# Two 128x128 by 256-column products that nobody reads, added to each of the 72 groups of a recurrence kernel

## The chip, the cores and the metric

The kernel runs on one core of one Trainium2 chip. The metric is device time in microseconds (us) of one execution; the time before is the median of 3 runs, 4142.04 us (4137.38 to 4148.01). Engines are named as the profile names them: PE is the matrix engine, PEld its weight loads, DVE, ACT and POOL the vector, scalar and general engines, SP the one that issues DMAs.

## The reference, cut to what matters

One layer of a trunk over 256 context and 2048 latent tokens of width 1024. A modulated norm and one input projection feed four mixers (mLSTM, RWKV-7, GLA, Gated DeltaNet) of 4 heads each. Every mixer scans the tokens forward and backward in chunks of 64; from chunk to chunk it carries a small state. For the DeltaNet heads, for example:

```python
def step(s, xs):
    u_c, w_c, k_c, ge = xs
    v_new = u_c - jnp.einsum('bhck,bhkv->bhcv', w_c, s)
    return jnp.exp(ge)[..., None, None] * s + jnp.einsum('bhck,bhcv->bhkv', k_c, v_new), s
```

The RWKV-7 step is of the same kind, with a triangular solve ahead of it. Then follow the output projection, a gated residual, a norm, a squared-ReLU MLP of width 4096, a second gated residual and a final norm:

```python
x = x + gate1_x * (mixed[:, n_ctx:] @ w_out[layer])
x = x + gate2_x * _mlp(_rms(x, norm2_w[layer]) * (1 + scale2_x) + shift2_x, mlp_w1[layer], mlp_w2[layer])
return _rms(x, final_norm_w)
```

## The kernel before, in words

**Dense work.** Every large product is split into a high and a low part in fp32r and made of three products of 128x128 weights by 512 (or 256) columns: `ps_z` is the input projection, `ps_o` the output projection, `ps_f` and `ps_a` the two halves of the MLP. `load_w` fetches a weight tile `w_f` by DMA, ACT makes `w_hi` of it and DVE or POOL `w_lo`.

**Rounds.** The tokens come in six rounds of chunks (`CHUNKS`). A round projects its tokens, prepares gates, decays and keys and writes them to DRAM; `solve` makes the triangular inverses of a chunk pair (`ps_n`, `ps_s`).

**Groups.** `group(d, c0)` makes one chunk of 64 tokens in one direction d for all four mixers: 36 chunks by 2 directions are 72 groups. Its products are in plain f32, 64x64 by 64 columns, of which two run on different halves of the array; each stands in the trace as two records. The chain from state to state is: products into `ps_R` from the old state `St`; then ACT copies columns 0 to 127 of it into `rR` and DVE makes `gR` of columns 128 to 255; products of both with the chunk's inverses (`X64`) into `ps_U`; ACT copies columns 0 to 255 into `U`; products into `ps_S`; POOL and DVE make the new `St`. `ps_R`, `ps_U` and `ps_S` are tiles of one pool tag, "ch", with one buffer of 128x512 f32, which is one PSUM bank: each of the three is opened when the readers of the one before are done. Columns 256 to 511 of `ps_R` and `ps_U` are not used. Beside the chain a group makes `ps_att` and `ps_ml` ahead of it, and the outputs `ps_ym` and `ps_ylgr` and, at its second direction, the norms and `ps_yT` behind it.

**What sets the order.** `interleave` in `body` writes the groups between the steps of the dense work: 48 of them during rounds 1 to 5, 24 during the first 35% of `tails`, the stage of output projection and MLP. What is written is then ordered by the tile framework: a planner plays the program through with its own costs (`schedule_with_timeline_sim=True`) and fixes, engine by engine, the order in which instructions stand; on the chip every engine runs its list in that order. `add_manual_dep(..., ORDER)` tells the planner that one instruction stands behind another on the same engine, without a wait. `self.ident` is a 128x128 identity, part of the constants' tile `pack`.

Of the kernel before, what the change touches and what calls it, by code (L numbers as in the profile page):

```python
# [166 lines left out]
ORDER = mybir.DependencyInfo(mybir.DependencyClass.NoSync, mybir.DependencyReason.DATA)  # L167
# [9 lines left out]
class Kern:  # L177
# [31 lines left out]
    def grp(self, t, par, mms):  # L209
# [6 lines left out]
                    self.tc.add_manual_dep(i.ins, p, ORDER, reason="one sum at a time in a bank")  # L216
        t.last[par] = i.ins.name

    def weave(self, t, mms):


        qs = [range(m[0].start // 32, m[0].stop // 32) for m in mms]
        left = collections.Counter(q for r in qs for q in r)
        for (rows, cols, l, r), quarters in zip(mms, qs):
            for q in quarters:
                left[q] -= 1
            prev = {t.last[q] for q in quarters if q in t.last}
            assert not prev or all(q in t.last for q in quarters)
            i = self.T.matmul(t.t[rows, cols], l, r, start=not prev, stop=not any(left[q] for q in quarters), skip_group_check=True)  # L229
            for p in prev:  # L230
                self.tc.add_manual_dep(i.ins, p, ORDER, reason="the first product of the bank's rows first")
            t.last.update({q: i.ins.name for q in quarters})
# [39 lines left out]
    def consts(self):  # L272
        A, c = self.A, self.ctx.enter_context(self.tc.tile_pool(name="const", bufs=1))
        self.cp = c
        pk = c.tile([128, sum(math.prod(x) for _, x in PACK)], F32, name="pack")
        self.dma(pk, A["pack"])
        v, o = {}, 0
        for k, x in PACK:
            w = math.prod(x)
            v[k] = pk[:, o:o + w]  # L280
            if len(x) == 2:
                v[k] = v[k].rearrange("p (a b) -> p a b", a=x[0])
            o += w
        self.vec = v
        self.ident, self.headsel, self.pairsel, rm = (v["k_" + k] for k in ("ident", "headsel", "pairsel", "rm"))
        self.rm64, self.rm16, self.rm4 = rm[:, 0:256], rm[:, 256:320], rm[:, 320:324]
        self.first = v["k_first"]
        for k in ("rw0", "ra0", "gconv", "nw"):
            self.ts(self.vec[k], self.vec[k], 0.5, ALU.mult)

        self.kah = c.tile([128, 2], F32, name="kah")
        self.ts(self.kah, self.vec["rka"], 0.5, ALU.mult)
        self.kac = c.tile([128, 2], F32, name="kac")
        self.ts(self.kac, self.kah, -1.0, ALU.mult, 1.0, ALU.add)

        self.rgn = c.tile([128, 2, 2, 128], F32, name="rgn")
        self.dma(self.rgn.rearrange("p x f d -> p (x f d)"), A["rgn"].to_broadcast([128, 512]))
        self.rc0 = c.tile([128, 8], F32, name="rc0")
        self.ts(self.rc0, self.vec["mup"], -1.0, ALU.mult, 1.0, ALU.add)
        self.tt(self.rc0, self.rc0, self.vec["mun"], ALU.subtract)  # L300
        self.mhalf = c.tile([128, 8], F32, name="mhalf")
        self.G.memset(self.mhalf, -0.5)
        self.ones = c.tile([128, 2], F32, name="ones")
        self.G.memset(self.ones, 1.0)
        self.pairq = c.tile([128, 2], F32, name="pairq")
        self.ts(self.pairq, self.pairsel, 32 ** -0.5, ALU.mult)
        self.reg = c.tile([128, 2, 2, NCH], F32, name="reg")
        self.leg = c.tile([128, 2, NCH], F32, name="leg")
        self.fs = [c.tile([128, NCH], F32, name=f"fs{d}") for d in range(2)]
# [1147 lines left out]
    def group(self, d, c0):  # L1457
# [9 lines left out]
        if hasq:  # L1467
            o, i = (13, 27) if d else (6, 0)
# [6 lines left out]
        r, i = self.part(c0)  # L1475
        i = X[f"rows{r}"][d, i].rearrange("h f k t -> h (f k t)")
        for h, p in enumerate(sl):
            self.dma(rw[p].rearrange("p f k t -> p (f k t)"), i[h:h + 1].to_broadcast([64, 640]))
        X64 = self.lt("t64", [2, 2, 64])
        i = X["t64"][d, c0 // 2].rearrange("p (m c w) -> p m c w", m=2, c=2)  # L1480
        self.dma(X64.rearrange("p m f t -> p m (f t)"), i[:, :, c0 % 2])
        tm = self.lt("tm", [1038])
        o = 332 if d else 0
# [7 lines left out]
        f2, g2 = sl, [slice(128, 192), slice(192, 256)]  # L1491
# [12 lines left out]
        b = self.bank(self.qa, "att", "ps_att", 1).t  # L1504
        rk = b[:, 0:256].rearrange("p (a t) -> p a t", t=64)
        ra, pk = (b[:, x:x + 128].rearrange("p (f t) -> p f t", f=2) for x in (256, 384))
# [37 lines left out]
        if hasq:  # L1544
# [4 lines left out]
            b = self.bank(self.qa, "att", "ps_ml", 1).t  # L1549
# [21 lines left out]
        def chb(nm):  # L1571
            return self.bank(self.qa, "ch", nm, 1)
        b = chb("ps_R")
# [2 lines left out]
        self.weave(b, [(p, f2[ft], Lt[p, 1 + ft], vr(ft)[p]) for ft, p in fp]  # L1576
                   + [(p, f2[ft], ff[p, 1 + ft], st[p, cr(ft)]) for ft, p in fp]
                   + [(p, g2[ft], kw[p, ft], st[p, f2[ft]]) for ft, p in fp])
        rR, gR = self.wt("rR", [128]), self.wt("gR", [128])
        self.act(rR, b.t[:, 0:128], AF.Copy)  # L1580
        self.tt(gR, vb, b.t[:, 128:256], ALU.add)
        b = chb("ps_U")
        for m, o, r in ((0, f2, rR), (1, g2, gR)):
            for ft, p in fp:
                self.mm(b.t[p, o[ft]], X64[p, m, ft], r[p, f2[ft]])

        U = self.wt("U", [256])
        self.act(U, b.t[:, 0:256], AF.Copy)
# [1 line left out]
        b = chb("ps_S")  # L1590
# [33 lines left out]
        for ms in ("m", "lgr"):  # L1624
            b = self.bank(self.qa, "yy", "ps_y" + ms, 1)
            first, then, last = [], [], []
            for mi, mm in enumerate(ms):
                w = 65 if mm == "m" else 64
                for ft, p in fp:
                    y = slice(128 * mi + w * ft, 128 * mi + w * ft + w)  # L1630
                    f, c, t, v = {"m": (Lq[:, 2 + ft], cm(ft), Lt[:, 6 + ft], vm(ft)), "l": (ff[:, 4 + ft], cl(ft), lS[:, ft], vl(ft)),
                                  "g": (Lq[:, ft], f2[ft], Lt[:, 4 + ft], U[:, g2[ft]]),
                                  "r": (ff[:, 3 * ft], cr(ft), Lt[:, 3 * ft], vr(ft))}[mm]
# [24 lines left out]
        else:  # L1658
            self.finish(yall, gat)
            b = self.psum("ps_yT", "yt" if "yt" in self.pb else "pp")  # L1660
# [271 lines left out]
```

## Time and profile before

| | |
|---|---|
| median of 3 runs | 4142.04 us |
| the profiled execution's own time | 4137.76 us |
| its span in the profile | 4136.0 us |
| PE busy | 3453.5 us (83%) |
| DVE, POOL, ACT busy | 2411.0, 1445.8, 1399.0 us |
| mean granted PE clock | 0.882 of full |

The span is the time between the first and the last recorded instruction; 1.8 us lie around it. "Busy" is the time in which an engine has an instruction under way, and PE's clock is told as the share of full speed that was granted. A pause of an engine is shown in brackets with what ended it.

### The profile page before, as it was taken

What the parts mean: (1) busy time and instruction counts of PE and PEld (TensorE: products, weight loads), DVE (VectorE), ACT (ScalarE), POOL (GpSimd) and SP (SyncE); (2) the same over time, 40 slices, a digit from 0 to 9 for tenths busy, and PEclk for the clock granted to TensorE, in tenths of its full rate; (3) what the DMA queues carried; (4) which work ended last, traced back from release to release, by engine and by line L of the source; (5) the groups of instructions that cost most, each with busy time, mean ns of one, the idle gap of its engine ahead of it and who ended that gap; (6) DMA issues with size and microseconds to landing.
All of it is one profiled execution on the core that took longest, in us unless ns stands there. A gap on an engine that the chain in (4) does not pass through costs nothing. (4 is left out here: it accounts for less than half of the span.)

```text
span 4136.0 us, 75041 instructions
## 1 busy us (share of the span) xinstructions
PE 3453.5 (83%) x29082; PEld 2794.0 (68%) x29082; DVE 2411.0 (58%) x5259; ACT 1399.0 (34%) x2544; POOL 1445.8 (35%) x1682
## 2 busy tenths in 40 slices
PE   6465878687777866568796999999999999999998
PEld 5344556566566755557685777777778778877886
DVE  6673875775587677536865645667653354335433
ACT  3334333443433433423332322233322332233222
POOL 3221735554345162502242423334422232223222
PEclk9667977877887886768898999999999999999999
DMA  5469577666776865757776544455622323232322
GB/s 203 112 182 146 107 157 182 162 133 157 146 158 138 196 140 144 171 142 196 195 215 183 160 123 143 139 153 150 196 91 97 114 94 124 97 107 92 104 97 86
DMA packets 609653, 592.68 MB, mean 143 GB/s; under 512 B 285664, under 2 KB 486448, under 8 KB 609296
## 3 DMA queue, kind: packets, MB, share of 16 engines
q1 hardware_dynamic: 609296, 587.87, 54.4%
q8 instruction: 230, 3.77, 0.4%
q14 instruction: 127, 1.04, 0.1%
HBM read 463.78 MB, written 123.92 MB: 142 GB/s over the span
## 5 line engine op out<-in xcount | busy, mean ns | idle before, releaser
L185 POOL TENSOR_TENSOR w_lo<-w_f,w_hi 128x1024 fp32r<-128x1024 f32 x213 | 511.6, 2402 | 1172.4 <-ACT w_hi L198 1086.2
L198 ACT ACTIVATE w_hi<-w_f 128x1024 fp32r<-128x1024 f32 (+1 forms) x427 | 448.0, 1051 | 956.8 <-PE ps_a L240 412.9
L185 DVE TENSOR_TENSOR w_lo<-w_f,w_hi 128x1024 fp32r<-128x1024 f32 (+1 forms) x214 | 269.8, 1261 | 248.4 <-ACT w_hi L198 245.8
L240 PE MATMUL ps_f<-h2h,w_hi 128*128 128x512 f32 x1024 | 404.5, 396 | 6.3 <-ACT w_hi L198 4.3
L240 PE MATMUL ps_a<-al,w_hi 128*128 128x512 f32 x1024 | 405.4, 396 | 0.0
L240 PE MATMUL ps_a<-ah,w_hi 128*128 128x512 f32 x1024 | 405.2, 401 | 0.0
L240 PE MATMUL ps_f<-h2h,w_lo 128*128 128x512 f32 x1024 | 404.8, 396 | 0.0
L240 PE MATMUL ps_a<-ah,w_lo 128*128 128x512 f32 x1024 | 402.6, 397 | 0.0
L240 PE MATMUL ps_f<-h2l,w_hi 128*128 128x512 f32 x1024 | 399.1, 394 | 3.5 <-DVE h2l L193 3.4
L240 PE MATMUL ps_z<-hh,w_hi 128*128 128x512 f32 (+3 forms) x760 | 306.2, 404 | 68.4 <-ACT hh L198 40.9
L193 DVE SCALAR_TENSOR_TENSOR x1T<-ps_a,modv,x1T 128x512 f32<-128x512 f32 x256 | 187.8, 748 | 279.9 <-PE ps_a L240 279.5
L240 PE MATMUL ps_z<-hh,w_lo 128*128 128x512 f32 (+3 forms) x760 | 301.1, 398 | 25.2 <-DVE w_lo L185 19.7
L240 PE MATMUL ps_z<-hl,w_hi 128*128 128x512 f32 (+2 forms) x760 | 294.8, 396 | 0.4 <-DVE hl L185 0.4
L240 PEld LDWEIGHTS ps_z<-hh,w_hi 128*128 128x128 f32 (+1 forms) x760 | 157.7, 208 | 110.2 <-ACT hh L198 46.1
L240 PEld LDWEIGHTS ps_f<-h2h,w_hi 128*128 128x128 f32 x1024 | 194.1, 190 | 51.4 <-ACT w_hi L198 6.9
L212 PE MATMUL ps_z<-w_hi,hh 128*128 128x256 f32 x672 | 206.3, 309 | 25.9 <-ACT w_hi L198 11.4
L240 PEld LDWEIGHTS ps_a<-ah,w_hi 128*128 128x128 f32 x1024 | 192.2, 188 | 50.0 <-DVE x1T L193 5.9
L240 PEld LDWEIGHTS ps_f<-h2l,w_hi 128*128 128x128 f32 x1024 | 193.8, 189 | 45.7 <-DVE h2l L193 4.7
L240 PEld LDWEIGHTS ps_a<-ah,w_lo 128*128 128x128 f32 x1024 | 192.5, 188 | 45.7 <-issue 0.5
L240 PEld LDWEIGHTS ps_f<-h2h,w_lo 128*128 128x128 f32 x1024 | 194.4, 190 | 41.4 <-DVE w_lo L185 0.5
L240 PEld LDWEIGHTS ps_a<-al,w_hi 128*128 128x128 f32 x1024 | 192.7, 188 | 43.8
L212 PE MATMUL ps_z<-w_lo,hh 128*128 128x256 f32 x672 | 203.3, 304 | 4.4 <-POOL w_lo L185 4.1
(430 smaller groups left out, 7835.1 us busy)
## 6 DMA issues: line engine op xcount, KB each, us to landing
w_f<-w SPq DMA_DIRECT2D x256, 512.0 KB
w_f<-wg SPq DMA_DIRECT2D x90, 512.0 KB
tm<-x_tm SPq DMA_DIRECT2D x144, 259.5 KB
kc<-x_fm SPq DMA_DIRECT2D x64, 448.0 KB
adaw<-ada SPq DMA_DIRECT2D x48, 512.0 KB
rw<-x_rows SPq DMA_DIRECT2D x144, 160.0 KB
w_f<-wp SPq DMA_DIRECT2D x44, 512.0 KB
w_f<-wout SPq DMA_DIRECT2D x32, 512.0 KB
```

The costliest lines, as they stand in the source:

```text
L185: return (e or self.V).tensor_tensor(out=o, in0=a, in1=b, op=op)
L193: return self.V.scalar_tensor_tensor(o, a, s, b, op0, op1)
L198: return self.S.activation(o, a, f, bias=bias, scale=scale)
L212: i = self.T.matmul(o, l, r, start=k == 0, stop=k == len(mms) - 1)
L240: return self.T.matmul(o, l, r, start=start, stop=stop)
```

## The change

A method `warm` is added. It makes one f32 product of the identity (128x128) with the first 256 columns of `pack`, into columns 256 to 511 of a bank that is just in use; no instruction reads them. A group calls it twice: behind the last product into `ps_R`, with all products into `ps_U` ordered behind it, and behind the last product into `ps_U`. What the kernel computes stays as it was.

```diff
+    def warm(self, t, after):
+
+        i = self.T.matmul(t.t[:, 256:512], self.ident, self.pack[:, 0:256], start=True, stop=True)
+        for p in after:
+            self.tc.add_manual_dep(i.ins, p, ORDER, reason="in the pause after")
+        return i.ins.name
...
+        self.pack = pk
...
         self.weave(b, [(p, f2[ft], Lt[p, 1 + ft], vr(ft)[p]) for ft, p in fp]
                    + [(p, f2[ft], ff[p, 1 + ft], st[p, cr(ft)]) for ft, p in fp]
                    + [(p, g2[ft], kw[p, ft], st[p, f2[ft]]) for ft, p in fp])
+        warm = self.warm(b, b.last.values())
         rR, gR = self.wt("rR", [128]), self.wt("gR", [128])
         self.act(rR, b.t[:, 0:128], AF.Copy)
         self.tt(gR, vb, b.t[:, 128:256], ALU.add)
         b = chb("ps_U")
         for m, o, r in ((0, f2, rR), (1, g2, gR)):
             for ft, p in fp:
-                self.mm(b.t[p, o[ft]], X64[p, m, ft], r[p, f2[ft]])
+                i = self.mm(b.t[p, o[ft]], X64[p, m, ft], r[p, f2[ft]])
+                self.tc.add_manual_dep(i.ins, warm, ORDER, reason="in the pause before")
+                b.last[ft, p.start, m] = i.ins.name
+        warm = self.warm(b, b.last.values())
```

The planner orders the whole program anew, so rows move on all engines, on SP too, by a few places each; no tile, pool or DMA is added or taken away. The first place is PE's list in one of the last groups before `tails`. Before:

```order
L229 MATMUL ps_R<-St,kw 64x64 x4
L240 MATMUL ps_ml<-kc 64x128 x2
L240 MATMUL ps_U<-rR,t_23576 64x64 x4
L240 MATMUL ps_U<-gR,t_23576 64x64 x4
L240 MATMUL ps_ml<-kc 32x128 x2
L240 MATMUL ps_ml<-kc 32x2x32 x2
L229 MATMUL ps_ym<-tm,Lt 64x65 x4
L229 MATMUL ps_S<-tm,mke 32x65 x4
```

and now:

```order
L236 MATMUL ps_R<-St,kw 64x64 x4
L221 MATMUL ps_R<-pack 128x256
L247 MATMUL ps_ml<-kc 64x128 x2
L247 MATMUL ps_U<-rR,t_23668 64x64 x4
L247 MATMUL ps_U<-gR,t_23668 64x64 x4
L221 MATMUL ps_U<-pack 128x256
L247 MATMUL ps_ml<-kc 32x128 x2
L247 MATMUL ps_ml<-kc 32x2x32 x2
L236 MATMUL ps_ym<-tm,Lt 64x65 x4
L236 MATMUL ps_S<-tm,mke 32x65 x4
```

The added product stands directly behind the chain's products, both times, and what stood in the pauses still stands there. The second place is PE's list in a group during `tails`, around `ps_U`. Before:

```order
L240 MATMUL ps_ml<-kc 32x128 x2
L229 MATMUL ps_ym<-tm,Lt 64x65 x3
L240 MATMUL ps_U<-rR,t_26330 64x64 x4
L240 MATMUL ps_U<-gR,t_26330 64x64 x4
L229 MATMUL ps_ym<-tm,Lt 64x65
L240 MATMUL ps_a<-ah,w_lo 128x512
```

and now:

```order
L247 MATMUL ps_ml<-kc 32x128 x2
L236 MATMUL ps_ym<-tm,Lt 64x65 x4
L247 MATMUL ps_a<-ah,w_lo 128x512
L247 MATMUL ps_U<-rR,t_26438 64x64 x4
L247 MATMUL ps_U<-gR,t_26438 64x64 x4
L221 MATMUL ps_U<-pack 128x256
L247 MATMUL ps_a<-ah,w_hi 128x512
```

The stretch behind the product is filled by the MLP's dense products, as it was.

One thing the lists don't tell stands in the built program's wait counts. A wait on PE is a wait for a count of finished products. Before, the copies `rR` and `U` wait for the count that the chain's last product brings; now, in all 72 groups, both wait for the count that the added product brings. The framework orders readers and writers by the bank, not by its columns, and the added product is written ahead of the copies.

## The prediction

> **What bounds the kernel now.** I read the page first for its totals and the slices of PE, then busy time by stage, then single groups.
>
> ```profile
> span 4136.0 us, 75041 instructions
> PE   6465878687777866568796999999999999999998
> PEclk9667977877887886768898999999999999999999
> PE 34%; DVE 1%; ACT 0%; POOL 0%; DMA 0%; issue 0%; POOLq 0%; DVEq 0%; ACTq 0%; SPq 0%
> ```
>
> PE's slices fall into two halves. From slice 23 on (about 2290 us) it is full at full clock, and the chain that ended last, which holds 35% of the span, is PE almost alone. Before that it is busy at six to eight tenths, and the granted clock is below full. The answer by stretches gives the stages: the first 424 us without a group, three stretches of the front with 50 groups, the tail's part with 22 groups, and the rest without.
>
> ```profile
> core 0: us, PE busy (x) PEld busy (x) DVE busy (x) ACT busy (x) POOL busy (x), PEclk, DMA share, GB/s
> 0.00:424.00 424.00, 239.52 (x1282) 192.49 (x1284) 256.83 (x683) 145.87 (x303) 118.47 (x197) 0.76 0.67 162
> 424.00:1000.00 576.00, 446.71 (x3951) 346.47 (x3949) 410.95 (x879) 220.23 (x441) 290.47 (x441) 0.80 0.68 148
> 1000.00:1500.00 500.00, 386.70 (x4341) 313.36 (x4337) 327.13 (x768) 185.65 (x376) 216.39 (x324) 0.82 0.73 162
> 1500.00:2290.00 790.00, 573.63 (x8359) 502.46 (x8360) 495.37 (x1385) 273.57 (x603) 257.51 (x357) 0.79 0.67 174
> 2290.00:3070.00 780.00, 769.87 (x6692) 601.86 (x6691) 479.05 (x1009) 239.97 (x391) 278.79 (x228) 0.99 0.48 145
> 3070.00:4136.00 1066.00, 1037.08 (x4475) 837.33 (x4473) 441.65 (x540) 333.74 (x432) 284.15 (x137) 0.99 0.31 101
> ```
>
> In the front (424 to 2290, 1866 us) PE is busy 446.71+386.70+573.63 = 1407 us, 75%, DVE 1233 us, 66%, and DMA runs at 0.67 to 0.73: three that take turns, none of which sets the stage alone. In the tail's group part PE is idle 10 us of 780: there every added microsecond of PE is one of the span. The count of groups comes from the copies of `ps_U` in the two windows:
>
> ```profile
> L198 ACT ACTIVATE U<-ps_U x50: 366/384/386, 538.1 to 2270.5; 128x256 f32<-128x256 f32 x50
> L198 ACT ACTIVATE U<-ps_U x22: 367/384/387, 2326.2 to 3061.5; 128x256 f32<-128x256 f32 x22
> ```
>
> **The price of one added product.** No f32 product of 128x128 by 256 columns is in the trace; the nearest has 64 rows instead of 128, the same 128 weight columns, 256 columns and type. It stands as two records; the time to the next row's start is what it takes of PE, shown here in one stretch at full and one at half clock.
>
> ```profile
> 559.65 0.70 PE L240 MATMUL ps_w<-wa,rwup 64*128 64x256 f32 x2
> 560.28 0.32 PE L229 MATMUL ps_S<-U,tm 64*64 64x64 f32 x2
> ...
> 541.67 1.22 PE L240 MATMUL ps_w<-wa,rwup 64*128 64x256 f32 x2
> 542.82 0.44 PE L229 MATMUL ps_S<-tm,mke 64*32 64x65 f32 x8
> ...
> 541.00:543.00 2.00, 2.00 (x14) 1.02 (x16) 0.00 (x0) 1.20 (x4) 0.00 (x0) 0.50 0.70 257
> 559.00:561.00 2.00, 1.59 (x9) 0.90 (x8) 1.97 (x6) 0.00 (x0) 0.00 (x0) 1.00 1.08 152
> ```
>
> 560.28-559.65 = 0.63 us at full clock, 542.82-541.67 = 1.15 at half; upper ends are the lengths 0.70 and 1.22 to the last record's end. A lower end is given by the fp32r products of 512 columns in the next fence: ten steps from 2493.54 to 2495.88, 0.234 us each, half of it for 256 columns, twice for two records: 0.23 us. I take 0.63 and 1.15, the row of the same type and width.
>
> **Term 1, the tail.** One of its groups, PE and ACT rows:
>
> ```profile
> 2492.87 0.41 PE L229 MATMUL ps_R<-St,kw 64*64 64x64 f32 x8
> 2493.21 0.50 PE L240 MATMUL ps_a<-ah,w_lo 128*128 128x512 f32 x1
> 2493.54 0.40 PE L240 MATMUL ps_a<-ah,w_hi 128*128 128x512 f32 x1
> 2495.88 0.40 PE L240 MATMUL ps_a<-al,w_hi 128*128 128x512 f32 x1
> 2496.83 0.34 PE L240 MATMUL ps_U<-rR,t 64*64 64x64 f32 x6
> ...
> 2493.32 0.28 ACT L198 ACTIVATE rR<-ps_R 128x128 f32<-128x128 f32 x1 [2.51 <-PE ps_R L229]
> ```
>
> The pause between `ps_R` and `ps_U` is no pause of PE: dense products start 0.34 us behind the last chain product and run on without a bracket. The copy `rR` is done at 2493.60, three microseconds before `ps_U`, so its later start (by one product) is covered by dense work. Covered, too, is the wait of what stands behind it on ACT and of `gR` on DVE. PE's own time is not covered. 22 groups x 2 x 0.63 = 27.7 us. Ends: 44 x 0.23 = 10 and 44 x 0.70 = 31.
>
> **Term 2, the front.** 50 groups x 2 = 100 products. A mean clock of 0.80 from full and half alone means that 40% of the time is at half: 100 x (0.6 x 0.63 + 0.4 x 1.15) = 84 us of PE (upper end with 0.70 and 1.22: 91). How much of that reaches the end? The same place of the program looks so in a front group:
>
> ```profile
> 2210.73 0.43 PE L229 MATMUL ps_R<-St,kw 64*64 64x64 f32 x8
> 2212.20 0.26 ACT L198 ACTIVATE rR<-ps_R 128x128 f32<-128x128 f32 x1
> 2212.93 0.28 DVE L185 TENSOR_TENSOR gR<-vb,ps_R 128x128 f32<-128x128 f32 x1
> 2213.27 0.45 PE L240 MATMUL ps_U<-rR,t 64*64 64x64 f32 x8 [1.06 <-DVE gR L185]
> 2213.55 0.40 PE L240 MATMUL ps_U<-gR,t 64*64 64x64 f32 x8
> 2213.99 0.38 ACT L198 ACTIVATE U<-ps_U 128x256 f32<-128x256 f32 x1 [1.47 <-PE ps_U L240]
> 2214.43 0.32 PE L229 MATMUL ps_S<-tm,mke 64*32 64x65 f32 x8 [0.48 <-ACT U L198]
> ```
>
> The first pause is set by ACT and DVE, which come to `rR` and `gR` late (2212.20, over a microsecond after `ps_R`): a product of 0.63 fits. The second is not: PE waits 0.48 us for `U`, and since that copy now waits for the product, the pause doesn't hide the product but begins behind it: +0.63, and DVE's and POOL's making of `St` comes as much later. So the product lies on the path where the chain of work runs through PE, and is absorbed where PE would have waited for DVE or DMA anyhow. With three parties sharing the stage I take a third: 28 us. Ends: 0 and 91.
>
> What PE waited for in the two pauses, next to its largest waits:
>
> ```profile
> PE ps_rb L248 <- ACT rb L198: 79.0, 23, 16.3
> PE ps_ke L248 <- DVE ke L185: 57.7, 19, 6.2
> PE ps_U L240 <- DVE gR L185: 16.4, 11, 4.3
> PE ps_S L229 <- ACT U L198: 1.9, 4, 0.8
> ```
>
> In 72 groups the two pauses held 16.4 + 1.9 = 18 us of waiting PE: mostly other products stand there already. Against 144 products of at least 0.63 us, some 90 us, this is the most that "in the pauses" could have hidden, if the copies didn't wait. The Trainium skill (PSUM — Partial Sum Buffer, section "PSUM bank collisions raise a hardware error") says that a reader and PE may not be in one bank and quadrant at once, disjoint columns included; no run here shows a collision. By that rule the waits are needed and the sum stands; without it up to 18 us would come off.
>
> **Term 3, the clock.** PE at half clock does its work at half speed: 0.40 x 1866 = 746 us of the front. The products add 100 x 0.63 = 63 us to a PE that idles 1866-1407 = 459 us, so they fill 14% of the idle time. If half-clock time shrank alike, 104 us would become full; PE, busy 75% of it, would need 39 us less, and by the third of term 2, 13 us would reach the end. Lower end: nothing, since the idle time lies at `ps_rb` and `ps_ke`, not in these pauses. I take 6.
>
> **Sum.** Against the profiled execution's own 4137.8 us (span 4136.0 and 1.8 around it; the runs' median is 4 us above, the lowest run just below): 4137.8 + 27.7 + 28 - 6 = 4187 us, +1.2%. The ends together: 4137.8 + 10 + 0 - 13 = 4135, and 4137.8 + 31 + 91 = 4260.
>
> **Rivals.**
> Only the tail pays. In the front the products all fall where PE waits for others; 459 us of idle PE speak for it, the 0.48 us pause against. 4137.8 + 27.7 - 6 = 4160.
>
> The recurrence sets the front. Its chain through state, `ps_R`, `ps_U`, `ps_S` is the longest path, every product lands in full: 4137.8 + 27.7 + 84 - 6 = 4243. Against it: 50 groups in 1866 us come every 37 us, and the quoted one takes 4 us from `ps_R` to `ps_S`; rounds fill the rest.
>
> The clock pays it back (the other side). Place: the front's half-clock time. Were it all gone, PE would save 0.75 x 746 / 2 = 280 us, a third of it 93; the products would cost 63 instead of 84, a third 21. With four fifths gone: 4137.8 + 27.7 + 22 - 75 = 4113. It decides from the point where more than about half is gone (47 us saved against 27.7 + 24). For it speaks that PE runs between six and eight tenths of clock in the whole front; against it, that the pauses quoted are a microsecond at most and already hold products. The Trainium skill (TensorE: Matmul & The Clock Gate, section "What's actually happening") names this mechanism: half rate after an idle window of about 3.4 us, full after a busy one. By that rule pauses this short don't lower the clock, and the trace agrees in the tail, 22 groups at 0.99.
>
> No change. The added work is there, but the planner's new order of the whole front wins back what it costs; rows moved by a few places on every engine, and 12% of the front's 459 us of PE waiting would do: 4140.
>
> **How the numbers follow.** Chances: forecast 0.53 (its own range 4155 to 4225), only the tail 0.14, the recurrence sets the front 0.10, the clock 0.15, no change 0.08. The measurement tells about 0.3%, 12 us, from no change. So faster 0.15, same 0.08, slower 0.53+0.14+0.10 = 0.77. The range 4133 to 4235 takes in the forecast, the tail's case and no change, and leaves out the clock's case and half of the recurrence's, 0.20. Its ends are about those of the sum; the upper one is cut, since all of the front's products landing is one case in ten.
>
> **What would show it.** Right: 288 new records on `ps_R` and `ps_U` with 256 columns, 0.63 us a pair at full clock; `rR` and `U` starting behind them; the stretch from the tail's first group to its last longer by about 28 us with PE full; the front longer by 10 to 60 us with its mean clock within 0.03 of 0.80. Wrong: a front clock of 0.9 or more, and a front that ends earlier than 2290; or a tail that did not grow, which would mean that dense products there had slack that the busy time hides.

## The result, and the profile after

| | before | changed |
|---|---|---|
| median | 4145.02 us (4137.38 to 4151.86, 4 runs) | 4193.02 us (4191.33 to 4198.7, 4 runs) |
| span of the profiled execution | 4136.0 us | 4189.6 us |
| mean granted PE clock | 0.882 | 0.883 |

The ratio is 1.0123, with a 95% interval from 1.011 to 1.0137: the change makes the kernel slower by 48 us. The forecast was 4187 us. The marks and spans below come from one profiled execution of each kernel; that of before took 4137.76 us, less than most of its runs, and differences between profiled executions lie up to 6 us off those between the medians.

First the changed kernel's page: the span, PE's slices and the engines of the chain that ended last.

```profile
span 4189.6 us, 75629 instructions
PE   6465889787777866768896999999999999999998
PE 40%; DVE 1%; DMA 1%; ACT 1%; POOL 0%; issue 0%; POOLq 0%; SPq 0%; DVEq 0%; ACTq 0%
```

588 more instructions: each of the 144 added products stands as two records on PE and two on the weight loads (576), and 12 are other records. The picture is the old one, a front of slices between 6 and 8 and a full tail. The next answer goes by stretches, whose borders I moved with the program (the columns are those of the prediction's second fence).

```profile
424.00:1000.00 576.00, 460.56 (x3833) 352.38 (x3832) 410.16 (x868) 219.83 (x438) 291.91 (x430) 0.80 0.65 146
1000.00:1500.00 500.00, 394.21 (x4474) 316.40 (x4474) 306.79 (x753) 180.71 (x370) 209.55 (x323) 0.83 0.72 161
1500.00:2320.00 820.00, 623.18 (x8543) 534.81 (x8542) 513.95 (x1410) 276.84 (x612) 275.82 (x371) 0.80 0.67 170
2320.00:3122.00 802.00, 789.53 (x6747) 614.05 (x6747) 480.16 (x1005) 240.84 (x391) 277.98 (x228) 1.00 0.47 141
3122.00:4189.60 1067.60, 1038.35 (x4522) 838.27 (x4516) 441.66 (x544) 333.90 (x432) 285.92 (x138) 0.99 0.30 101
```

The front holds 30 us more and the tail's groups 22, and the stage without groups is 1067.6 us against 1066. The clock of each stretch is within 0.01 of what it was. To place the loss in every kernel alike I take two marks from one row, the copies `U`: the start of the 50th (the last group of the front) and of the 72nd (the last of all).

```profile
L198 ACT ACTIVATE U<-ps_U x50: 357/384/388, 540.4 to 2300.1; 128x256 f32<-128x256 f32 x50
L198 ACT ACTIVATE U<-ps_U x22: 360/384/387, 2360.3 to 3115.8; 128x256 f32<-128x256 f32 x22
```

Against 2270.5 and 3061.5 of before, the front ends 29.6 us later and the last group 54.3 us later: 24.7 us are lost between the two.

The group that the prediction quoted, in the tail, looks so now; PE's rows, then ACT's.

```profile
2492.46 0.41 PE L236 MATMUL ps_R<-St,kw 64*64 64x64 f32 x8
2492.80 0.70 PE L221 MATMUL ps_R<-pack 128*128 128x256 f32 x2
2493.15 0.59 PE L247 MATMUL ps_f<-h2h,w_lo 128*128 128x512 f32 x1
2493.57 0.40 PE L247 MATMUL ps_f<-h2h,w_hi 128*128 128x512 f32 x1
...
2493.54 0.28 ACT L198 ACTIVATE rR<-ps_R 128x128 f32<-128x128 f32 x1
...
2498.24 0.38 ACT L198 ACTIVATE U<-ps_U 128x256 f32<-128x256 f32 x1 [0.97 <-PE ps_U L221]
```

The product follows the chain directly, dense work follows the product, and the copy `U` waits 0.97 us, until the product (L221) is done. PE has no bracket: it never stops. From the chain's last product to the second dense one are 2493.57-2492.46 = 1.11 us; before, in the prediction's rows, 2493.54-2492.87 = 0.67. The product takes 0.44 us here, not 0.63. What follows it here is a dense product; where small products follow, it costs more, as a later experiment shows.

### The profile page after: what moved, and what is told of

It reads as the page before. It is cut to its first block, busy times and chain, and to the rows that moved or that the text cites. A ratio compares the mean times of both kernels' runs of the same rounds, so it can differ in the third digit from the quotient of the medians.

```text
span 4189.6 us, 75629 instructions
## 1 busy us (share of the span) xinstructions
PE 3543.4 (85%) x29370; PEld 2847.2 (68%) x29370; DVE 2409.1 (58%) x5259; ACT 1397.4 (33%) x2544; POOL 1459.3 (35%) x1682
```

## The experiments

The theory of the prediction: in the tail each product costs PE's own time, in the front it costs where the chain of a group is the path. The rival that came up as the runs went on: the planner's new order costs, and the products little. All marks in one table, as differences from the profiled execution of before; the last column is the second mark less the first.

| run | span | 50th `U` | 72nd `U` | between |
|---|---|---|---|---|
| the change | +53.6 | +29.6 | +54.3 | +24.7 |
| `tail_only` | +21.0 | +6.7 | +26.5 | +19.8 |
| `front_only` | +29.4 | +29.2 | +30.1 | +0.9 |
| `two_columns` | +45.7 | +32.0 | +48.0 | +16.0 |
| `doubled` | +53.5 | +18.6 | +55.5 | +36.9 |
| `nudge_c` | +17.3 | +13.1 | +19.8 | +6.7 |
| `nudge_a` | -8.0 | +0.5 | -3.9 | -4.4 |
| `nudge_b` | +11.1 | +12.2 | +16.1 | +3.9 |
| `other_bank` | +82.8 | +66.8 | +85.5 | +18.7 |
| `old_order` | +39.0 | +20.6 | +42.3 | +21.7 |
| `old_order_two` | +26.3 | +18.3 | +31.8 | +13.5 |
| `new_order_none` | +29.7 | +20.7 | +29.3 | +8.6 |
| `before_again` (the same program) | +2.6 | +3.0 | +5.1 | +2.1 |

The last row is a control: two profiled executions of one program stand up to 5 us apart at these marks.

**One part alone.** The products only in the 24 groups that are written during `tails`, or only in the 48 before them:

```diff
     def warm(self, t, after):
+        if not hasattr(self, "A2"):      # front_only: if hasattr(self, "A2")
+            return None
...
```

> The two products only in the 24 groups that are written into the tails, none in the 48 before. PE's list is that of the kernel before up to the first product. Theory (PE's own time in a stage that PE fills): the front ends as before, and the whole is 19 to 28 us longer, 44 to 48 products of 0.43 to 0.63 us. Rival (dense products have slack there that the busy time hides): under 10 us. Rival (the new order moves the tail as well): a difference outside 15 to 32 us.

> The two products only in the 48 groups before the tails. PE's list is that of the changed kernel up to the tails. Theory (a part of the products lies on the path in the front): 25 to 35 us longer than before, all of it before the first product of the tails, so that this run's difference and that of the run with the tail alone add up to the change's 48 to 54. Rival (front and tail cover for each other): the sum is off by more than 15 us.

Measured: 4163.58 us, ratio 1.0062 (1.0042 to 1.0082), with the products in the tail; 4166.93 us, ratio 1.006 (1.0042 to 1.0077), with those in the front.

With the tail's products alone the loss lies behind the front (19.8 of 26.5 us), with the front's alone ahead of the tail (29.2 of 30.1). The two spans add to 50.4 us of the change's 53.6. So front and tail are two losses, each with its own place. What makes the front's is not told by this: `front_only` has the planner's new order there as well as the products.

**The product's size.** 2 columns in place of 256, with the same waits; and two products of 256 columns in place of one.

```diff
-        i = self.T.matmul(t.t[:, 256:512], self.ident, self.pack[:, 0:256], start=True, stop=True)
+        i = self.T.matmul(t.t[:, 256:258], self.ident, self.pack[:, 0:2], start=True, stop=True)
```

> As the change, but each added product has 2 columns instead of 256; the waits of the copies and the places in the lists stay as the change makes them, the planner orders anew. Theory (PE's time): most of the cost goes; tail under 8 us, front under 12 us, the whole under 20 us. Rival (order and waits, not the product's length): the front stays 25 us or more behind the kernel before.

> As the change, but two products of 256 columns in each place, four in a group. Theory (PE's time): twice the cost, 90 to 110 us over the kernel before, tail about 45, front 45 to 65. Rival (the clock pays back): the mean clock of the front rises from 0.80 to 0.84 or more and the second pair costs less than half of the first. Rival (order): the front's part is not twice that of the change, but anything from 0 to 60.

Measured: 4182.63 us, ratio 1.0094 (1.0074 to 1.0114), with 2 columns; 4194.91 us, ratio 1.0132 (1.0112 to 1.0152), doubled. Behind the front the loss goes with the size: 16.0, 24.7, 36.9 us. In the front it doesn't: 32.0, 29.6, 18.6 us. A share of PE's own time, by which the prediction sized the front, should have grown there. Either something else than the product's length costs in the front, or the order, which the planner makes anew for the doubled products, hides it.

**How much an order alone can do.** 2-column products in a single group: the first, the seventh, the 22nd. That is less than a microsecond of PE.

```diff
+        if (self.ngr[0], self.ngr[1]) != (1, 0):      # nudge_a: (4, 2), nudge_b: (7, 14)
+            return None
...
```

> The products with 2 columns, and only in the first of the 72 groups: half a microsecond of work in all. The planner orders anew from there on. Theory (the front's 28 us are the new order, not the products): the front ends 10 us or more away from the kernel before, to either side. Rival (the copies wait for a product in each of 48 front groups): the front within 5 us of the kernel before, as one wait of under 1 us can't do more; the whole within 5 us.

> As the run with the products in the first group, but in the seventh group instead. Theory (new order): the front again 10 us or more away from the kernel before, and by another amount than the nudge of the first group. Rival (waits in each group): within 5 us.

> As the run with the products in the first group, but in the 22nd, where 26 front groups are still to come. Theory (new order): unchanged up to about 1240 us, then away from the kernel before by several microseconds, to either side. Rival (waits in each group): within 5 us everywhere.

Measured: 4155.71 us, ratio 1.0032 (1.0021 to 1.0043), in the first group; 4138.95, ratio 0.9991 (0.9982 to 1.0001), in the seventh; 4156.69, ratio 1.0042 (1.0025 to 1.0059), in the 22nd. In the traces 53, 56 and 32% of PE's records stand at another place than in before, and 63% with the whole change (the added products left out). Two of three new orders cost some 15 us for less than a microsecond of work (4155.71 and 4156.69 against 4141.23), and the third costs nothing at the end, though its single copies `U` in the front lie between 11.7 us ahead of before's and 15.6 behind. So a comparison of two orders carries 15 us or more that belong to no product, and in a new order a single copy doesn't tell how far the front has come. `nudge_a` is the only kernel here that isn't slower than before, and its interval holds no change.

**Without the wait.** The products go into the bank of the outputs (`ps_ym`), which is opened ahead of `ps_R`, so that the copies wait for the chain alone.

```diff
+        spare = self.bank(self.qa, "yy", "ps_ym", 1)
...
-        warm = self.warm(b, b.last.values())
+        warm = self.warm(spare, b.last.values())
```

> As the change, 256 columns in all 72 groups, but the products go into the bank of the outputs, which is opened ahead of the chain for it; the copies rR and U wait for the chain's products alone, and the planner orders anew. Theory (waits of the copies make the front's 28 us): front under 10 us behind the kernel before, tail about as in the change, 20 to 28; whole 20 to 38. Rival (PE's time): front and tail as in the change, 48 to 54. Rival (order): tail 20 to 28, front anything from -20 to 60.

Measured: 4221.8 us, ratio 1.0187 (1.0169 to 1.0206), the slowest of all. It doesn't answer the question. Its first copy `U` starts at 704.0 us instead of 538.1, so the order has moved far, and in the waits of PE `ps_S` for `U` grows to 13.4 us from the 1.9 of the prediction's fence. The likely reason, not shown, is that the early opening ties the chain to whoever read that bank before, so that one wait goes and others come.

**The order held.** The answer needs the products without the planner's order, and the order without the products. For this the order of a built program is written into the kernel as a table, and each instruction is tied behind the one ahead of it in its engine's list; a product is put directly behind the chain's products that it follows. With the table of before and no product the program is that of before, instruction by instruction.

```diff
             body(ctx, tc, A, out)
+            fixed_order(tc, list(nc.cur_bb.bb.instructions), WARM)
...
+        for a, b in zip(seq, seq[1:]):
+            tc.add_manual_dep(b, a.name, ORDER, reason="fixed order")
```

> The change with its 144 products, but with every engine's list held, instruction by instruction, in the order of the kernel before; each product stands directly behind the chain's products. What is left of the change is the products' own time and the copies' wait for them; the planner's new order is gone. Theory A, the products and the waits cost what the changed kernel shows: first ps_o product 25 to 32 us later than before, end 45 to 55 us later (span 4181 to 4191). Theory B, the front's 29 us come from the new order: first ps_o within 8 us of before, tail 19 to 25 us longer, end 17 to 33 us later (span 4153 to 4169).

> The same in the order of the kernel before, with 2 columns in place of 256, so that the waits are the same and the product is short. Theory A by waits: first ps_o 25 to 30 us later, as with 256 columns. Theory A by the product's length: first ps_o less than half as late as in the run with 256 columns. Theory B: first ps_o within 8 us of before, tail 10 to 15 us longer (44 products of 0.23 us), end 2 to 23 us later (span 4138 to 4159).

> The kernel before, without any added product, with every engine's list held in the order that the planner made for the changed kernel. Theory A, the products and waits cost: within 6 us of before everywhere (span 4130 to 4142). Theory B, the order costs: first ps_o 20 to 30 us later, tail within 5 us of before, span 4155 to 4170.

> A control: the kernel before with every engine's list held in its own order, which is the same program instruction by instruction. It tells how far two profiled executions of one program stand apart at the marks that the other runs are compared by. Every theory that reads 10 us or more as an effect needs less than that here: span within 6 us of 4136.0, every mark of the front and the tail within 5 us of the profiled execution of the kernel before. If the marks differ by 10 us or more, the comparisons in the front tell nothing.

Measured: the change in before's order 4180.28 us, ratio 1.0091 (1.0076 to 1.0106); the same with 2 columns 4169.76, ratio 1.007 (1.0053 to 1.0087); the changed kernel's order without products 4168.58, ratio 1.0063 (1.0046 to 1.008). The control had one run, 4140.41 us, its marks within 5.1 us; single runs of before lie between 4130.61 and 4151.86 us, so one execution alone can be further off than that. The change in before's order, then with 2 columns:

```profile
L232 ACT ACTIVATE U<-ps_U x50: 365/384/388, 541.0 to 2291.1; 128x256 f32<-128x256 f32 x50
L232 ACT ACTIVATE U<-ps_U x22: 384/385/386, 2348.1 to 3103.8; 128x256 f32<-128x256 f32 x22
```

```profile
L232 ACT ACTIVATE U<-ps_U x50: 365/384/387, 538.5 to 2288.8; 128x256 f32<-128x256 f32 x50
L232 ACT ACTIVATE U<-ps_U x22: 366/385/387, 2346.0 to 3093.3; 128x256 f32<-128x256 f32 x22
```

The first `ps_o` product, by which the expectations go, starts 22.4, 20.1 and 19.8 us later than before, in the order of the list above. Neither theory holds by itself. The products and the copies' waits cost 39.0 us in an order that didn't move, 20.6 of them in the front; the order costs 29.7 us without any product, 20.7 of them in the front. Together they don't cost the sum, 68.7, but 53.6: in the front two delays of about 20 us make one of 29.6. The medians say the same: 36.7 and 25.0 us over the runs of before beside them, where the change has 48.0. That is as it would be in a stage with slack, where a part of each delay falls into time that the other has already lost. Why the new order is worse by itself is open, and the copies don't tell where in the front its delay arises, since the groups themselves stand at other places in it: the 26th copy comes 19.5 us later than before's, the 30th 7.3 us earlier, the 50th 20.7 later.

**The tail at a fixed order.** The same place of the group again, in before's order with 256 columns and then with 2 (PE's rows):

```profile
2517.12 0.41 PE L271 MATMUL ps_R<-St,kw 64*64 64x64 f32 x8
2517.46 0.70 PE L255 MATMUL ps_R<-pack 128*128 128x256 f32 x2
...
2518.23 0.39 PE L282 MATMUL ps_a<-ah,w_hi 128*128 128x512 f32 x1
```

```profile
2514.17 0.41 PE L271 MATMUL ps_R<-St,kw 64*64 64x64 f32 x8
2514.51 0.38 PE L255 MATMUL ps_R<-pack 128*128 128x2 f32 x2
...
2515.07 0.39 PE L282 MATMUL ps_a<-ah,w_hi 128*128 128x512 f32 x1
```

1.11 and 0.90 us against 0.67 of before: the product takes 0.44 us with 256 columns and 0.23 with 2. That holds ahead of a dense product, where 25 of the tail's 44 stand. The group's second product stands ahead of small ones; before, and in before's order with 256 columns:

```profile
2497.07 0.34 PE L240 MATMUL ps_U<-gR,t 64*64 64x64 f32 x6
...
2497.79 0.39 PE L240 MATMUL ps_a<-ah,w_hi 128*128 128x512 f32 x1
```

```profile
2521.74 0.40 PE L282 MATMUL ps_U<-gR,t 64*64 64x64 f32 x7
2522.07 0.70 PE L255 MATMUL ps_U<-pack 128*128 128x256 f32 x2
2522.70 0.33 PE L271 MATMUL ps_ym<-tm,Lt 64*64 64x65 f32 x2
...
2523.29 0.39 PE L282 MATMUL ps_a<-ah,w_hi 128*128 128x512 f32 x1
```

From the chain's product to the second dense one are 2523.29-2521.74 = 1.55 us against 2497.79-2497.07 = 0.72: here the product costs 0.83 us, of which 0.63 (2522.70-2522.07) pass until the next row starts. Over all 44, PE's busy time between the marks grows from 778.3 to 802.5 us, 24.2 us or 0.55 a product; 21.7 of it come out at the second mark, and 2.5 fall into PE's idle time there (12.7 us before, 10.2 now). With 2 columns it is 15.5 us of PE and 13.5 at the mark; the control has 0.3 and 2.1. The tail is settled: PE's own time, and nothing else of size.

**The front at a fixed order.** Where do the 20 us arise? Before's copies up to the 35th group, and the seven after that:

```profile
L198 ACT ACTIVATE U<-ps_U x35: 366/384/386, 538.1 to 1950.8; 128x256 f32<-128x256 f32 x35
L198 ACT ACTIVATE U<-ps_U x7: 366/384/384, 1977.0 to 2105.3; 128x256 f32<-128x256 f32 x7
```

With the change in before's order, and with 2 columns:

```profile
L232 ACT ACTIVATE U<-ps_U x35: 365/384/388, 541.0 to 1959.8; 128x256 f32<-128x256 f32 x35
L232 ACT ACTIVATE U<-ps_U x7: 367/384/386, 1986.2 to 2124.6; 128x256 f32<-128x256 f32 x7
```

```profile
L232 ACT ACTIVATE U<-ps_U x35: 365/384/387, 538.5 to 1956.3; 128x256 f32<-128x256 f32 x35
L232 ACT ACTIVATE U<-ps_U x7: 366/384/384, 1984.3 to 2121.5; 128x256 f32<-128x256 f32 x7
```

35 groups lose 9.0 us (5.5 with 2 columns); the next seven lose as much again, from +9.0 to +19.3 (from +5.5 to +16.2). The control has -0.3 at the 35th copy and +0.3 at the 42nd. Those seven stand 21 us apart, (2105.3-1977.0)/6, against 42 us before them, (1950.8-538.1)/34: where groups come this close, a delay in one may still be there when the next begins, which is a reading and not shown by itself. In the change itself this place isn't seen, since the order there is another: its copies are 27.6 us late at the 35th already, 27.5 at the 42nd and 29.6 at the 50th.

One of the seven in before, DVE's rows by time and then POOL's, and the same instructions with the change in before's order, with rows of PE and ACT ahead of them:

```profile
2006.23 0.29 DVE L185 TENSOR_TENSOR ga<-rw,tm 128x128 f32<-128x128 f32 x1 [0.49 <-DMA tm<-x_tm]
2006.44 0.28 DVE L185 TENSOR_TENSOR vb<-tm 128x128 f32<-128x128 f32 x1
2006.64 0.28 DVE L185 TENSOR_TENSOR ke<-tm 128x128 f32<-128x128 f32 x1
2006.85 0.22 DVE L185 TENSOR_TENSOR mke<-tm 128x64 f32<-128x64 f32 x1
2006.98 1.35 DVE L185 TENSOR_TENSOR md<-rw,tm 128x128 f32<-128x128 f32 x1
...
2006.90 1.29 POOL L185 TENSOR_TENSOR xh<-xh,rbr 128x512 f32<-128x512 f32 x1 [1.57 <-DMA xh<-xT]
```

```profile
2013.38 1.22 PE L255 MATMUL ps_R<-pack 128*128 128x256 f32 x2
2014.53 0.69 PE L282 MATMUL ps_ml<-kc 64*64 64x128 f32 x4
...
2017.59 0.38 ACT L232 ACTIVATE U<-ps_U 128x256 f32<-128x256 f32 x1 [1.10 <-PE ps_U L255]
...
2018.93 0.29 DVE L219 TENSOR_TENSOR ga<-rw,tm 128x128 f32<-128x128 f32 x1
2019.14 1.36 DVE L219 TENSOR_TENSOR vb<-tm 128x128 f32<-128x128 f32 x1
2020.42 1.35 DVE L219 TENSOR_TENSOR ke<-tm 128x128 f32<-128x128 f32 x1
2021.69 1.28 DVE L219 TENSOR_TENSOR mke<-tm 128x64 f32<-128x64 f32 x1
2022.90 1.36 DVE L219 TENSOR_TENSOR md<-rw,tm 128x128 f32<-128x128 f32 x1
...
2017.78 6.34 POOL L219 TENSOR_TENSOR xh<-xh,rbr 128x512 f32<-128x512 f32 x5 [2.48 <-DMA xh<-xT]
```

The product takes 2014.53-2013.38 = 1.15 us here, at half clock, and `U` waits for the second one. DVE comes to `ga` 12.70 us later than before, and POOL to its first `xh` only 10.88 later, since `xh` waits for a transfer and not for the group. So DVE's block, which stood ahead of `xh`, now stands beside it: `vb`, `ke` and `mke` take 1.36, 1.35 and 1.28 us in place of 0.28, 0.28 and 0.22, and `md` comes 15.92 us later. The collision adds 3.2 us (15.92-12.70) to a group in which the copy `U` had come 2.4 us later than in the group before it (+12.6 against +10.2). With 2 columns the same block collides too: `ga` comes 10.01 us later than before and `md` 14.12. The control shows that this needs no product. It jumps from +0.3 to +3.9 us between the 42nd and the 43rd copy; DVE there, in the control:

```profile
2112.01 0.29 DVE L219 TENSOR_TENSOR kw<-kc,rw 128x128 f32<-128x128 f32 x1 [1.82 <-DMA kc<-x_fm]
...
2112.22 2.45 DVE L219 TENSOR_TENSOR ke<-tm 128x128 f32<-128x128 f32 x1
```

A transfer lands a microsecond later than in before (`kw` starts at 2110.98 there), `ke` falls beside a long `w_lo` of POOL and takes 2.45 us in place of 0.54, 1.9 of the jump's 3.6 us.

Collisions are not the whole of it. Up to the 50th copy DVE is busy 1218 us in before, 1223 with 256 columns, 1225 with 2 and 1220 in the control, for the same list of instructions, so longer DVE instructions can make up some 5 of the 20 us. PE tells more: up to that copy it is busy 1390 us in before, 1442 with 256 columns and 1437 with 2, while its idle time falls from 456 to 425 and 427. Of 51 and 47 us of added PE time 31 and 29 went into idle time, and 21 and 18 came through. Which waits these passed along was not followed, and whether the front pays for PE's time or for the copies' waits stays open, since both lengths add nearly the same PE time.

## Why the prediction came out right, step by step

**What bounds the kernel.** Right: a full tail, and a front in which three engines take turns.

**The waits.** Right: the brackets above show `U` waiting for the product (L221 and L255), and at the fixed order ACT waits for it 51 times before `rR` and 63 times before `U`, in 72 groups.

**Price of a product.** At half clock 1.15 us was right. At full clock 0.63 was a little too much as a mean: PE's time in the tail grew by 0.55 a product. The row `ps_w` from which 0.63 came has small f32 products behind it, and there the step to the next row is 0.63 again, though the whole cost is 0.83. I read it as a price that holds whatever follows. Ahead of a dense product it is 0.35 us to the next row's start (2492.80 to 2493.15) and 0.09 more at the step after that (0.42 against 0.33), 0.44 in all.

**Term 1, the tail, 27.7 us.** Mechanism right, size a little too high. By the price it would be 44 x 0.55 = 24.2 us of PE; 2.5 of them fell into the 12.7 us that PE was idle, which the term had put at nothing, and 21.7 came out (19.8 with the tail's products alone). The change as a whole shows 24.7; a few microseconds of the order (8.6 without any product) may be in it.

**Term 2, the front, 28 us.** At a fixed order 20.6 us, of which up to 3 are the control's. What the clock did is in this number, so it stands against terms 2 and 3 together, 28 - 6 = 22. That they come so near is in part luck: PE's added time was 51 us and not 84, and 0.4 of it came through and not a third. Nor is it spread as a share: the first 42 groups bring 19.3 us of delay, and the last seven of these 10.3. "Absorbed where PE would have waited for DVE or DMA anyhow" holds, 31 us of PE's idle time were filled. What the term lacked is that a delay can grow by collision, by 3.2 us in the one group that was followed. And it priced the front by PE's time at a given clock, while the loss hardly follows the product's length (18.3 us with 2 columns, 20.6 with 256).

**Term 3, the clock, -6 us.** The sign of the effect is there. The front (its window 10 to 20 us longer in the last three) of before, of before's order with 2 columns, with 256, and of the doubled products in their own order:

```profile
424.00:2290.00 1866.00, 1407.03 (x16643) 1162.29 (x16640) 1233.44 (x3029) 679.46 (x1419) 764.37 (x1121) 0.80 0.69 163
```

```profile
424.00:2310.00 1886.00, 1456.56 (x16827) 1211.41 (x16826) 1238.46 (x3024) 680.02 (x1418) 764.26 (x1120) 0.79 0.68 161
```

```profile
424.00:2310.00 1886.00, 1458.36 (x16853) 1189.32 (x16851) 1235.27 (x3027) 681.79 (x1420) 763.03 (x1122) 0.81 0.68 161
```

```profile
424.00:2300.00 1876.00, 1462.55 (x17013) 1199.60 (x17013) 1219.07 (x3014) 675.47 (x1411) 762.36 (x1120) 0.84 0.68 161
```

PE is busy for 1457, 1458 and 1463 us with 2, 256 and twice 256 columns: the clock goes from 0.79 to 0.81 to 0.84 as the products grow, and their length hardly shows. In before's order the products' own records take 45 us up to the 50th copy with 2 columns and 86 with 256, and yet PE's total grows by only 4 us: the rest of its work took 1380 us instead of 1408. All four runs of each show the step, over the whole execution: a mean clock of 0.876 to 0.879 with 2 columns, 0.885 to 0.887 with 256. Against before the change itself moves the clock by 0.01, so the gain that the term stood for isn't visible as a gain; it is the likely reason why a long product costs the front hardly more than a short one. That the clock caused this is read from these runs, of which the doubled one has another order, and not from a run that held the clock.

**What the sum left out.** The new order was in the prediction only as a rival that wins back the whole cost. The runs show it with the other sign and as large as the front's term: 29.7 us by itself. On PE "a few places each" understated it: half of the moved records moved by more than 20 places, some by 500. The three terms made 49.7 us, where the products by themselves cost 39.0; the order brings 14.6 on top of that. So the total was right to 6 us by luck: the terms were too high by about 11, nearly all of it in the tail (where 3.3 us also come back behind the last group, +42.3 at its mark and +39.0 at the end), and the missing one put 15 back.

**The rivals.** Only the tail pays: out, since at a fixed order the products cost the front 20.6 us (the 29.4 of `front_only` hold the new order too). The recurrence sets the front: out, since not every product landed in full, 20.6 us where it had 84; in the seven close groups the loss is the same with 2 columns as with 256, so it isn't the products' length there either. The clock pays it back: at most in part. No change: out.

## What to carry to other kernels

Work that fills a pause is only free if nobody waits for it: here it shared a bank with the copies that end the pause, and they waited. Price an added instruction by what follows it (0.44 us ahead of a dense product, 0.83 ahead of small ones), in the full stage by PE's own time between two rows, and in a stage with slack look for the groups that stand closest together. Where a planner orders the program, hold its order before you ascribe ten or twenty microseconds to an edit, since less than a microsecond of work moved this kernel by some 15.

## What was unexpected of the hardware

A 128x128 by 2-column f32 product takes 0.23 us between small and dense products, more than half of the 0.44 that 256 columns take: most of a short product is its fixed part.

DVE's 128x128 `TENSOR_TENSOR` took 0.28 us alone and 1.35 beside POOL's `xh`; four in a row, one of them 128x64, took 1.28 to 1.36, each about as long as one `xh` (6.34/5 = 1.27 us). The Trainium skill (SBUF — State Buffer, section "Who interferes with whom") says that DVE and GpSimd share one pair of ports under an exclusive lock. The trace agrees: each of the four ends about one POOL instruction after the one before it (they start at 2019.14, 2020.42, 2021.69 and 2022.90), so that between two of POOL's just one of DVE's gets in.
